# Padding the rows of weight, input and squared-activation buffers of a two-layer encoder kernel

## The chip, the cores and the metric

The kernel runs on one core of one Trainium2 chip. The metric is the device time of one execution in microseconds (us), as a median of repeated runs. Beside it stands one profiled execution, from which every duration of a single instruction is read.

Engine names as in the profile: PE is TensorE doing matrix products, PEld is TensorE loading the stationary operand of a product, DVE is VectorE, ACT is ScalarE, POOL is GpSimd, SP is SyncE, which issues most DMA transfers. A name such as L125 is a line of the kernel file.

## What is computed

The reference is a small sequence model in float32: 512 tokens, width 1024, two layers, each a token mixer and an MLP, both with a norm ahead and a residual behind.

```python
for i in range(DEPTH):                       # DEPTH = 2
    h = _rmsnorm(x, norm_mix[i])
    if i % 2 == 0:                           # differential attention and pooling
        ...
        x = x + jnp.concatenate([a_out, b_out], axis=-1) @ ab_w_out[e]
    else:                                    # gated linear attention
        x = x + _gla_mixer(h, gla_w_in[o], ..., gla_w_out[o])
    h = _rmsnorm(x, norm_ffn[i])
    x = x + jnp.square(jax.nn.relu(h @ ffn_w1[i])) @ ffn_w2[i]   # 1024 -> 4096 -> 1024
return _rmsnorm(x, norm_final)
```

Nearly all arithmetic lies in products with weights. The two MLPs alone hold 2 x 2 x 1024 x 4096 weights.

## The kernel before

**Products in three passes.** A weight product is made from float32r operands. Each operand is split in a high part and a low part: `wh` and `wl` for weights, `ah` and `al` for inputs. Each product is then the sum of three matrix products, `wh*ah + wh*al + wl*ah`. They are the lines L125, L126 and L127 of the helper `mm3`. The stationary operand is a block of 128x128 of `wh` or `wl`; it is loaded by an LDWEIGHTS ahead of its own product, while the product before it still runs. The moving operand is a whole tile `ah` or `al` with 512 columns, one for each token.

**One output tile.** `proj_T` makes 128 output features for all tokens: it goes over eight blocks `kb` of 128 input features, three products each, so 24 products go to one PSUM bank. `proj_tok` (L150 to L152) makes the opposite layout for the attention values, with `ah` or `al` stationary and `wh` or `wl` moving.

**Weights.** `Stream.next` hands out halves of a unit of 1 MB. The unit is loaded by a DMA from SP into one of two `wraw` buffers. `split_w` makes `wh` on ACT (L103) and `wl` on DVE (L104). There are four `wh` and four `wl` buffers of 1024 numbers each, so several halves are ready ahead.

**The MLP** (`ffn`). In four chunks, eight output tiles of the first weight are made from the 8 pairs `ah`, `al`. Each result is put through relu and squared and split in two tiles of the row `r16` (L425 to L428), so a chunk fills 16 tiles of `r16`. Then eight output tiles of the second weight are made with these `r16` tiles as moving operands. In the very last chunk (`last_chunk`) this second half is done in two halves of 256 tokens. So the program has long stretches in which PE reads `ah` and `al`, and stretches of 192 products in which it reads `r16`. Trace names cut off buffer numbers, so `r16` and `r8` both appear as `r`.

**Layer mixers.** Attention and pooling in layer 0, gated linear attention in layer 1, are made of weight products with other, smaller products put between them (for instance sums over partitions, L182 and L183, which multiply a temporary tile with the ones matrix `onesr`). The low-rank gate of layer 1 (L522) is a run of 16 products whose stationary operand is an `r8` tile and whose moving operands are `ah` and `al`.

**Order and places.** A tile scheduler orders each engine's instructions; `soon` raises the priority of what PE waits for. Buffers of one tag form a row in SBUF, a fixed stretch of bytes in each partition; the rows stand one behind the other, and a tag's buffers have equal distances. The allocation helper is

```python
def T(shape, tag, bufs, dt=F32):
    cnt[0] += 1
    return sb.tile(shape, dt, tag=tag, bufs=bufs, name=f"{tag}_{cnt[0]}")
```

`w_tiles` asks it for `wh` and `wl` (4 buffers of 4096 bytes each per partition), `act_tiles` for `ah` and `al` (12 of 2048 bytes each), `row16` for `r16` (16 of 2048 bytes). All these sizes are multiples of 512 bytes, so all buffers of a row begin at the same remainder modulo 512. In the built program the remainders are 128 for every buffer of `wh`, `wl`, `ah` and `al`, also for `tmp` and `onesr`, and 256 for every buffer of `r8` and `r16`. A 128x128 block within `wh` or `wl` begins a multiple of 512 bytes behind its buffer's start.

Of the kernel before, what the change touches and what calls it, by code (L numbers as in the profile page):

```python
# [17 lines left out]
S = 512  # L18
# [9 lines left out]

# columns of the packed parameter array
C_MIX0, C_FFN0, C_MIX1, C_FFN1, C_FIN = 0, 8, 16, 24, 32  # L30
# [5 lines left out]
def trunk(ctx: ExitStack, tc: tile.TileContext, xT, par, lvl, lam4, wqk0, wu0, wv0, poolw, wo0,  # L36
          wgk, wup, wqk1, wv1, wg1, wo1, w1a, w2a, w1b, w2b, outT):
    nc = tc.nc
# [3 lines left out]
    cnt = [0]  # L42

    def T(shape, tag, bufs, dt=F32):
        cnt[0] += 1
        return sb.tile(shape, dt, tag=tag, bufs=bufs, name=f"{tag}_{cnt[0]}")

    # buffers by how long they are held: a row of 8 and a row of 16
    def row8(n=S, dt=F32):
# [17 lines left out]

    # what the tensor engine waits for goes ahead of the rest
    def soon(n=300):
        return tc.high_priority(n)  # L70

    # ---- parameters, inputs and the first unit of weights
    prm = T([P, N_PAR], "par", 1)
# [16 lines left out]

    # ---- weight streaming: raw float32 units, split into two parts of 12 bits
    def load(src):
# [14 lines left out]
    class Stream:  # L107
        """Halves of the units of one weight array, in order."""

# [19 lines left out]
    def proj_T(w, act, ts=slice(0, S)):  # L129
        """[128 features, tokens] from a half unit [128, 8, 128] and split inputs."""  # L130
        hi, lo = w
        ps = PS("mm", (P, ts.stop - ts.start))
        for kb in range(KB):
            c = slice(kb * P, (kb + 1) * P)
            ah, al = act[kb]
            mm3(ps, (hi[:, c], lo[:, c]), (ah[:, ts], al[:, ts]), kb == 0, kb == KB - 1)
        return ps

    def proj_tok(stream, act):
        """Four [128 tokens, 512 features] results from half units [128, 2, 512]."""  # L140
        pss = [PS("mm") for _ in range(NT)]
        for pair in range(KB // 2):
            wh, wl = stream.next()
            for t in range(NT):
                ts = slice(t * P, (t + 1) * P)
                for j in range(2):
                    kb = 2 * pair + j
                    c = slice(j * S, (j + 1) * S)
                    ah, al = act[kb]
                    PE.matmul(pss[t], ah[:, ts], wh[:, c], start=kb == 0, stop=False)  # L150
                    PE.matmul(pss[t], al[:, ts], wh[:, c], start=False, stop=False)  # L151
                    PE.matmul(pss[t], ah[:, ts], wl[:, c], start=False, stop=kb == KB - 1)  # L152
        return pss

    def split_scaled(src, col):
        """Parts of src * (a value per partition)."""
        ah, al = act_tiles()
        A.activation(ah, src, AF.Copy, scale=col)
        V.scalar_tensor_tensor(out=al, in0=src, scalar=col, in1=ah.bitcast(F32), op0=ALU.mult, op1=ALU.subtract)
        return ah, al  # L160
# [7 lines left out]
    def spread(r):  # L168
        """Values per token [128, n] along the free axis of every partition, in PSUM."""
        n = r.shape[-1]  # L170
        ps = PS("ax", (P, n * P))
        for t in range(n):
            PE.matmul(ps[:, t * P:(t + 1) * P], r[:, t:t + 1].to_broadcast([P, P]), ident, start=True, stop=True)
        return ps

    def col_sums(sq, c):
        """Sums over all partitions, on every partition, of a tile to which c is added."""
        n = sq.shape[-1]
        ps, hi, lo = PS("ax", (P, n)), tmp(n, F32R), tmp(n, F32R)
        A.activation(hi, sq, AF.Copy)  # L180
        V.scalar_tensor_tensor(out=lo, in0=sq, scalar=c, in1=hi.bitcast(F32), op0=ALU.add, op1=ALU.subtract)
        PE.matmul(ps, ones_r, hi, start=True, stop=False)  # L182
        PE.matmul(ps, ones_r, lo, start=False, stop=True)  # L183
        return ps
# [7 lines left out]
    def rsqrt(r, v, inv):  # L192
        """(v * inv) ** -0.5: a first value by logarithm, then one Newton step."""
        A.activation(r, v, AF.Ln, scale=inv)
        A.activation(r, r, AF.Exp, scale=-0.5)
        return newton(r, v, inv, tmp(r.shape[-1]))

    def neg_recip(r, v, inv):
        """-1 / (v * inv), in the same way."""
        t = tmp(r.shape[-1])  # L200
        A.activation(r, v, AF.Ln, scale=inv)
        A.activation(r, r, AF.Exp, scale=-1.0)
        V.scalar_tensor_tensor(out=t, in0=v, scalar=inv, in1=r, op0=ALU.mult, op1=ALU.mult)
        V.scalar_tensor_tensor(out=r, in0=t, scalar=-2.0, in1=r, op0=ALU.add, op1=ALU.mult)
        return r

    class Norm:
        """Sums of squares over the features of x, tile by tile."""

# [24 lines left out]
    def per_token(rb):  # L234
        """One row of rb as [128 tokens, 4]."""
        ps = PS("ax", (P, NT))
        for t in range(NT):
            PE.transpose(ps[:, t:t + 1], rb[0:1, t * P:(t + 1) * P], ident[0:1, 0:1])
        r = T([P, NT], "rtok", 1)
        V.tensor_copy(r, ps)  # L240
        return r

    # ================= layer 0: attention and pooling =================
    act = []
# [16 lines left out]
    rb = nrm.rb()  # L261

    # lambda on every partition
    l4 = tmp(256)
# [25 lines left out]
    def scores(h, qts):  # L290
        """Score blocks of 128 queries each, masked, in two banks; minus their scaled maxima."""
        banks = [PS("ax"), PS("ax")]
# [18 lines left out]
    def softmax(h, qt, views, neg):  # L311
        """p1 - lambda * p2, transposed, into the head's tiles."""
        n = (qt + 1) * P
# [29 lines left out]
    def attend(h):  # L343
        """The products with the values, normalised."""
        po = PS("ax")
# [26 lines left out]

    # pooling branch
    pw = tmp2().rearrange("p (g c) -> p g c", g=4)
# [24 lines left out]
    def add_out(arr, src, col):  # L399
        """x += (split inputs) @ weights; the next block's inputs and norm."""  # L400
        st = Stream(arr)
# [50 lines left out]
    def last_chunk(s2, a, rb2):  # L452
        """The end of the last block by halves of the tokens, each with its final norm."""
        for half in range(2):
# [34 lines left out]

    # constants of layer 1  # L490
    lv = T([P, NLEV + 1, P], "lvl", 1, U8)
# [10 lines left out]

    # ================= layer 1: gated linear attention =================
    with soon(800):
        smask = row8()
        G.memset(smask, 1.0)
        G.memset(smask.rearrange("p (c t) -> p c t", t=P)[:, :, 0:1], 0.0)
        # gate weights: both parts of the 16 columns side by side, so two passes make all the products;
        # four copies of them, for the stacked product of the up-projection
        gk2 = [row8(dt=F32R).rearrange("p (k a b) -> p k a b", k=4, a=4) for _ in range(2)]  # L510
        for i in range(2):
            src = gkr[:, 4 * i:4 * i + 4, :, :]
            A.activation(gk2[i][:, :, :, 0:16], src, AF.Copy)
            V.tensor_tensor(gk2[i][:, :, :, 16:32], src, gk2[i][:, :, :, 0:16].bitcast(F32), ALU.subtract)
        # rows 0-63: the weights' high part, rows 64-95: the low part
        wu = row8(dt=F32R)
# [7 lines left out]
    rb = nrm.rb()  # L524
    # rows 0-31 and 64-95: the high part of the gate's input, rows 32-63: the low part
    gkf = tmp2()
# [37 lines left out]
    def weights(h):  # L564
        """Products within chunks, and the factors across them, of one head."""
        ps = proj_T(st.next(), act)
# [8 lines left out]
        b3 = b.rearrange("p (c t) -> p c t", t=P)  # L575
        # across chunks
        e = row16()
# [16 lines left out]
        kdt.append(kd)  # L594
        # within chunks: the diagonal, then pairs (second half, first half) of ever smaller blocks
        at = row16()
# [6 lines left out]
        for l in range(NLEV - 1):  # L603
# [12 lines left out]
            if s >= 16:  # L616
                # whole blocks, which start at partitions that a product can be put at
                for p0 in range(0, P, 2 * s):
# [7 lines left out]
            for c in range(NT):  # L626
# [3 lines left out]
                              psl.rearrange("p (c t) -> p c t", t=P))  # L630
        # neighbours, as the diagonal: the products' sums over the features
        d = tmp(S // 2)
# [23 lines left out]
    def outputs(h):  # L656
        """Transposed outputs of one head, normalised: two tiles [128 features, tokens]."""
        half, hh = divmod(h, 2)
# [34 lines left out]

    # the parts of the heads, in the order that keeps every engine supplied
    for h in range(3):
# [28 lines left out]

# ---- layout on the host
def _blocks_T(w):
    """Rows in blocks of 1024, columns in units of 256: [units, 128, 2, 8 * 128]."""
    k, n = w.shape
# [4 lines left out]
def _blocks_tok(w):  # L733
    """Columns in blocks of 512, rows in units of 512: [units, 128, 2, 2 * 512]."""
    n = w.shape[1]
# [64 lines left out]
```

## Time and profile before

| | us |
|---|---|
| median of 3 runs | 1136.92 |
| lowest and highest run | 1136.45, 1137.26 |
| span of the profiled execution, first to last instruction | 1135.0 |
| PE busy | 1118.5 |
| PEld busy | 904.5 |
| DVE busy | 641.5 |
| ACT busy | 468.2 |
| POOL busy | 7.2 |

The profiled execution is one run; its time is its span and the little that lies ahead of and behind the instructions. Its span is 1.9 us under the median of the runs. Busy time of PE counts the stretch in which any product is under way. One product is recorded with about 0.39 us, but products overlap in the pipeline: the next one begins 0.23 us later. What counts for the time is therefore the distance from one product's start to the next one's start; it is called the **pitch** below, and is read from the timeline, which prints starts to 0.01 us.

### The profile page before, as it was taken

What the parts mean: (1) busy time and instruction counts of PE and PEld (TensorE: products, weight loads), DVE (VectorE), ACT (ScalarE), POOL (GpSimd) and SP (SyncE); (2) the same over time, 40 slices, a digit from 0 to 9 for tenths busy, and PEclk for the clock granted to TensorE, in tenths of its full rate; (3) what the DMA queues carried; (4) which work ended last, traced back from release to release, by engine and by line L of the source; (5) the groups of instructions that cost most, each with busy time, mean ns of one, the idle gap of its engine ahead of it and who ended that gap; (6) DMA issues with size and microseconds to landing.
All of it is one profiled execution on the core that took longest, in us unless ns stands there. A gap on an engine that the chain in (4) does not pass through costs nothing.

```text
span 1135.0 us, 13269 instructions
## 1 busy us (share of the span) xinstructions
PE 1118.5 (99%) x5312; PEld 904.5 (80%) x5312; DVE 641.5 (57%) x1024; ACT 468.2 (41%) x748; POOL 7.2 (1%) x26
## 2 busy tenths in 40 slices
PE   8999999999999999999999999999999999999996
PEld 6676778888888888888777788888888888888896
DVE  7757866423433455456898867555323434455485
ACT  7445544323322422334645466434323313312463
POOL 0000000000000000000000000000000000000001
PEclk9999999999999999999999999999999999999998
DMA  7221233232222323222121312232232323223252
GB/s 247 80 90 38 84 109 111 74 111 79 107 103 84 111 74 111 81 106 92 58 75 38 113 38 74 74 112 88 98 109 77 111 74 112 91 96 107 79 187 75
DMA packets 19229, 107.21 MB, mean 94 GB/s; under 512 B 2048, under 2 KB 5120, under 8 KB 7008
## 3 DMA queue, kind: packets, MB, share of 16 engines
q1 hardware_dynamic: 19024, 106.34, 26.9%
q8 instruction: 42, 0.69, 0.2%
q14 instruction: 19, 0.16, 0.0%
q10 hardware_dynamic: 144, 0.03, 0.0%
HBM read 104.26 MB, written 2.10 MB: 94 GB/s over the span
## 4 chain that ended last, share of the span: by engine, by line
PE 92%; DVE 2%; issue 2%; ACT 2%; DMA 1%; SPq 0%; POOL 0%; POOLq 0%; DVEq 0%; ACTq 0%
PE psmm L127 26%; PE psmm L126 26%; PE psmm L125 26%; PE psmm L150 2%; PE psmm L152 2%; PE psmm L151 2%; PE psax L301 1%; PE psax L628 1%; PE psax L621 1%; PE psax L347 1%; DMA wraw<-in_wqk 1%; PE psax L182 1%; PE psax L678 0%; PE psax L663 0%; PE psax L329 0%
## 5 line engine op out<-in xcount | busy, mean ns | idle before, releaser
L103 ACT ACTIVATE wh<-wraw 128x1024 fp32r<-128x1024 f32 x190 | 200.9, 1059 | 517.6 <-PE psmm L126 480.1
L104 DVE TENSOR_TENSOR wl<-wraw,wh 128x1024 fp32r<-128x1024 f32 x190 | 232.2, 1223 | 264.3 <-ACT wh L103 263.6
L125 PE MATMUL psmm<-ah,wh 128*128 128x512 f32 x864 | 339.6, 393 | 4.9 <-ACT wh L250 4.9
L126 PE MATMUL psmm<-al,wh 128*128 128x512 f32 x864 | 339.4, 393 | 0.0
L127 PE MATMUL psmm<-ah,wl 128*128 128x512 f32 x864 | 338.9, 392 | 0.0
L126 PE MATMUL psmm<-r,wh 128*128 128x512 f32 (+1 forms) x576 | 213.0, 370 | 0.1
L125 PE MATMUL psmm<-r,wh 128*128 128x512 f32 (+1 forms) x576 | 213.1, 370 | 0.0
L127 PE MATMUL psmm<-r,wl 128*128 128x512 f32 (+1 forms) x576 | 213.0, 370 | 0.0
L125 PEld LDWEIGHTS psmm<-ah,wh 128*128 128x128 f32 x864 | 162.7, 188 | 41.1 <-ACT wh L250 5.6
L126 PEld LDWEIGHTS psmm<-al,wh 128*128 128x128 f32 x864 | 162.7, 188 | 36.5 <-issue 2.1
L127 PEld LDWEIGHTS psmm<-ah,wl 128*128 128x128 f32 x864 | 162.8, 188 | 35.7 <-issue 1.6
L126 PEld LDWEIGHTS psmm<-r,wh 128*128 128x128 f32 x576 | 108.2, 188 | 20.7 <-DVE r L428 0.3
L127 PEld LDWEIGHTS psmm<-r,wl 128*128 128x128 f32 x576 | 108.2, 188 | 20.4
L125 PEld LDWEIGHTS psmm<-r,wh 128*128 128x128 f32 x576 | 108.1, 188 | 20.4
L439 DVE TENSOR_TENSOR r<-r,psmm 128x512 f32<-128x512 f32 x32 | 22.0, 687 | 88.7 <-PE psmm L127 88.7
L428 DVE TENSOR_TENSOR r<-tmp,r 128x512 fp32r<-128x512 f32 x64 | 44.3, 692 | 6.5
L427 DVE TENSOR_TENSOR tmp<-tmp 128x512 f32<-128x512 f32 x64 | 43.8, 684 | 0.0
L426 ACT ACTIVATE r<-tmp 128x512 fp32r<-128x512 f32 x64 | 40.5, 634 | 2.0
L150 PE MATMUL psmm<-wh,ah 128*128 128x512 f32 x96 | 39.1, 407 | 0.0
L151 PE MATMUL psmm<-wh,al 128*128 128x512 f32 x96 | 38.5, 401 | 0.0
L152 PE MATMUL psmm<-wl,ah 128*128 128x512 f32 x96 | 38.2, 398 | 0.0
L425 ACT ACTIVATE tmp<-psmm 128x512 f32<-128x512 f32 x64 | 36.9, 577 | 0.0
(183 smaller groups left out, 813.0 us busy)
## 6 DMA issues: line engine op xcount, KB each, us to landing
wraw<-in_w2b SPq DMA_DIRECT2D x20, 1024.0 KB, 4.8
wraw<-in_w1a SPq DMA_DIRECT2D x16, 1024.0 KB, 4.8
wraw<-in_w2a SPq DMA_DIRECT2D x16, 1024.0 KB, 4.8
wraw<-in_w1b SPq DMA_DIRECT2D x16, 1024.0 KB, 4.8
wraw<-in_wo SPq DMA_DIRECT2D x8, 1024.0 KB, 4.7
wraw<-in_wqk SPq DMA_DIRECT2D x7, 1024.0 KB, 4.9
wraw<-in_wv SPq DMA_DIRECT2D x6, 1024.0 KB, 4.7
wraw<-in_wg SPq DMA_DIRECT2D x4, 1024.0 KB, 4.9
```

Of the source, the lines that this page charges most:

```text
L103: A.activation(hi, src, AF.Copy)
L104: V.tensor_tensor(lo, src, hi.bitcast(F32), ALU.subtract)
L125: PE.matmul(ps, wh, ah, start=first, stop=False)
L126: PE.matmul(ps, wh, al, start=False, stop=False)
L127: PE.matmul(ps, wl, ah, start=False, stop=last)
L150: PE.matmul(pss[t], ah[:, ts], wh[:, c], start=kb == 0, stop=False)
L151: PE.matmul(pss[t], al[:, ts], wh[:, c], start=False, stop=False)
L152: PE.matmul(pss[t], ah[:, ts], wl[:, c], start=False, stop=kb == KB - 1)
L425: A.activation(r, ps, AF.Relu)
L426: A.activation(hi, r, AF.Square)
L427: V.tensor_tensor(q, r, r, ALU.mult)
L428: V.tensor_tensor(lo, q, hi.bitcast(F32), ALU.subtract)
```

## The change

The helper `T` takes a table of paddings, in numbers of 4 bytes. A buffer of `wh` and `wl` gets 16 numbers (64 bytes) more than its 1024, a buffer of `ah`, `al` and `r16` 24 numbers (96 bytes) more than its 512. The tile handed out is a slice without the padding. To make room, the area in SBUF that is kept for descriptors of DMAs issued by GpSimd shrinks from 16384 to 2048 bytes per partition. This kernel issues its DMAs from SP and ACT.

```diff
+    PAD = {"wh": 16, "wl": 16, "ah": 24, "al": 24, "r16": 24}
+
     def T(shape, tag, bufs, dt=F32):
         cnt[0] += 1
-        return sb.tile(shape, dt, tag=tag, bufs=bufs, name=f"{tag}_{cnt[0]}")
+        pad = PAD.get(tag)
+        if pad is None:
+            return sb.tile(shape, dt, tag=tag, bufs=bufs, name=f"{tag}_{cnt[0]}")
+        p, n = shape
+        full = {"wh": 1024, "wl": 1024}.get(tag, S) + pad
+        return sb.tile([p, full], dt, tag=tag, bufs=bufs, name=f"{tag}_{cnt[0]}")[:, 0:n]
...
-    nc = bacc.Bacc("TRN2", target_bir_lowering=False, num_devices=1)
+    nc = bacc.Bacc("TRN2", target_bir_lowering=False, num_devices=1, dynamic_dma_scratch_size=2048)
```

The rest of the diff takes out comments and docstrings. Lines of the helpers move down by 8: `mm3` is L133 to L135 afterwards, `split_w` L111 and L112.

In the built programs every engine has the same instructions in the same order with the same waits, before and after. What differs are start addresses in SBUF:

| row | start modulo 512 before | start modulo 512 after |
|---|---|---|
| `wh` (4) | 128 | 128, 192, 256, 320 |
| `wl` (4) | 128 | 384, 448, 0, 64 |
| `ah` (12) | 128 | 128, 224, 320, 416, 0, 96, 192, 288, 384, 480, 64, 160 |
| `al` (12) | 128 | 256, 352, 448, 32, 128, 224, 320, 416, 0, 96, 192, 288 |
| `r16` (16) | 256 | 0, 96, 192, 288, 384, 480, 64, 160, 256, 352, 448, 32, 128, 224, 320, 416 |
| `r8` (8) | 256 | 0 |
| `tmp`, `onesr`, `wraw`, `x` | 128 | 384, 128, 128, 128 |

A number that is used below is the **distance**: the start of the moving operand of a product minus the start of the stationary operand that is loaded while this product runs (that of the next product), modulo 512 bytes. Counted over the built programs:

```
products of float32r                     distance before           distance after
moving operand 512 columns, not r16      0: 2848 of 2865           all 16 multiples of 32, each 133 to 255 of 2865
moving operand r16, 512 columns          128: 1343 of 1344         all 16 multiples of 32, each 73 to 96 of 1344
moving operand r16, 256 columns          128: 380 of 380           15 of the 16 multiples of 32, each 11 to 48 of 380
```

Of the 17 others of the first row, 16 have distance 384: they stand around the gate's run L522, whose moving operands lie at 128 and whose stationary ones lie at 256.

## The prediction

> **What bounds the kernel now.** I read the page first: span, busy times, clock, and the chain of work that ended last.
>
> ```profile
> span 1135.0 us, 13269 instructions
> PE 1118.5 (99%) x5312; PEld 904.5 (80%) x5312; DVE 641.5 (57%) x1024; ACT 468.2 (41%) x748; POOL 7.2 (1%) x26
> PEclk9999999999999999999999999999999999999998
> PE 92%; DVE 2%; issue 2%; ACT 2%; DMA 1%; SPq 0%; POOL 0%; POOLq 0%; DVEq 0%; ACTq 0%
> ```
>
> PE is busy 99% of the span and is 92% of the chain, at full granted clock but for the last slice. So time is won or lost only where the pitch of the products changes, that is the distance from one start to the next. The groups of instructions (count, busy time and mean of one, then the idle time before them and its releaser) say which products these are, and whether the splitting of the weights is in their way.
>
> ```profile
> L103 ACT ACTIVATE wh<-wraw 128x1024 fp32r<-128x1024 f32 x190 | 200.9, 1059 | 517.6 <-PE psmm L126 480.1
> L104 DVE TENSOR_TENSOR wl<-wraw,wh 128x1024 fp32r<-128x1024 f32 x190 | 232.2, 1223 | 264.3 <-ACT wh L103 263.6
> L125 PE MATMUL psmm<-ah,wh 128*128 128x512 f32 x864 | 339.6, 393 | 4.9 <-ACT wh L250 4.9
> L125 PE MATMUL psmm<-r,wh 128*128 128x512 f32 x448 | 176.9, 395 | 0.0
> L125 PE MATMUL psmm<-r,wh 128*128 128x256 f32 x128 | 36.1, 283 | 0.0
> ```
>
> L126 and L127 have as many as L125: 3 x 864 = 2592 products with `ah` or `al` moving, 3 x 448 = 1344 with `r16`, 3 x 128 = 384 of half length. L125 never waits but for 4.9 us at the start, whereas L103 waits 517.6 us, 480.1 of them for PE to give a buffer back. The splits run ahead of PE.
>
> The third view is the timeline of PE alone, at the place where the first MLP goes over from `ah` and `al` to `r16` (start, duration, instruction):
>
> ```profile
> 223.51 0.39 PE L126 MATMUL psmm<-al,wh 128*128 128x512 f32 x1
> 223.74 0.39 PE L127 MATMUL psmm<-ah,wl 128*128 128x512 f32 x1
> 223.97 0.40 PE L125 MATMUL psmm<-r,wh 128*128 128x512 f32 x1
> 224.20 0.39 PE L126 MATMUL psmm<-r,wh 128*128 128x512 f32 x1
> 224.42 0.40 PE L127 MATMUL psmm<-r,wl 128*128 128x512 f32 x1
> 224.66 0.39 PE L125 MATMUL psmm<-r,wh 128*128 128x512 f32 x1
> 224.89 0.40 PE L126 MATMUL psmm<-r,wh 128*128 128x512 f32 x1
> 225.13 0.39 PE L127 MATMUL psmm<-r,wl 128*128 128x512 f32 x1
> 225.36 0.40 PE L125 MATMUL psmm<-r,wh 128*128 128x512 f32 x1
> ```
>
> Ahead of 223.97 the steps are 0.23; behind it 0.23, 0.22, 0.24, 0.23, 0.24, 0.23: another rhythm, that swings between two values. Over whole stretches (start and end, their length, then busy time and count on PE, PEld, DVE, ACT and POOL, clock, DMA share and GB/s) this gives exact pitches:
>
> ```profile
> 269.45:312.29 42.84, 42.84 (x190) 35.47 (x189) 18.86 (x22) 16.09 (x24) 0.00 (x0) 1.00 0.29 98
> sum 459.00, PE 459.00 PEld 380.07 DVE 232.93 ACT 187.61 POOL 0.00; mean PE 57.38 PEld 47.51 DVE 29.12 ACT 23.45 POOL 0.00
> 223.97:268.76 44.79, 44.79 (x194) 36.05 (x192) 11.10 (x10) 13.00 (x18) 0.00 (x0) 1.00 0.27 94
> sum 313.53, PE 313.53 PEld 252.29 DVE 132.59 ACT 84.14 POOL 0.63; mean PE 44.79 PEld 36.04 DVE 18.94 ACT 12.02 POOL 0.09
> ```
>
> The first row is eight output tiles of a first MLP weight, without their first three products: 8 x 24 - 3 = 189 products in 42.84 us, a pitch of **226.7 ns** (the 190th counted began before the stretch). The first sum is over eight such stretches, all with nothing but this even rhythm: 459.0 us, so 459.0 / 0.2267 = 2025 products. The third row is eight output tiles of a second weight: 192 products in 44.79 us, **233.3 ns**. The last row adds up all seven such stretches, 1344 products.
>
> One engine, one clock, instructions of one shape, no wait, and yet two pitches. What differs is the place of the operands: by the table of the change the distance is 0 in the one kind and 128 in the other. The gate's run has it the other way round, stationary at 256 and moving at 128:
>
> ```profile
> 533.97 0.39 PE L522 MATMUL psmm<-al,r 128*128 128x512 f32 x1
> 534.20 0.40 PE L522 MATMUL psmm<-ah,r 128*128 128x512 f32 x1
> 534.44 0.39 PE L522 MATMUL psmm<-al,r 128*128 128x512 f32 x1
> 534.67 0.40 PE L522 MATMUL psmm<-ah,r 128*128 128x512 f32 x1
> ```
>
> Steps of 0.23, 0.24, 0.23: the swinging rhythm, with `ah` and `al` moving. So it is not a matter of `r16`, but of the two places taken together. I read this as the loading of the next stationary operand getting in the way of the stream of the moving one, by an amount that hangs on the distance.
>
> At distance 0 the even rhythm has to be found first. Behind an interruption it looks like this:
>
> ```profile
> 564.91 0.40 PE L127 MATMUL psmm<-ah,wl 128*128 128x512 f32 x1
> 565.14 0.40 PE L125 MATMUL psmm<-ah,wh 128*128 128x512 f32 x1
> 565.38 0.39 PE L126 MATMUL psmm<-al,wh 128*128 128x512 f32 x1
> 565.60 0.39 PE L127 MATMUL psmm<-ah,wl 128*128 128x512 f32 x1
> ...
> 567.23 0.39 PE L127 MATMUL psmm<-ah,wl 128*128 128x512 f32 x1
> ```
>
> There are ten steps from 564.91 to 567.23 (the rows between begin at 565.83, 566.07, 566.29, 566.53, 566.76 and 566.99), so the mean is **232 ns**, with single steps from 0.22 to 0.24. All ten have distance 0. Only then come the steps of 226.7. So 226.7 is no property of one product: it is a state that a row of products of one and the same distance falls into, and stays in.
>
> **The change part by part.** No instruction, order or wait changes. The work is priced by the pitch alone.
>
> *Products with `ah` or `al` moving.* After the change their distance takes all 16 multiples of 32 evenly and is another one at nearly every product, so a state that needs one lasting distance is not reached. Only distances 0, 128 and 384 are in this trace; for the 13 others there is no row. Bounds from the nearest rows, where the trace holds starts to 1 ns: 224 ns (the least step, from 224.20 to 224.42, shown as 0.22) and 238 ns (the greatest, from 224.42 to 224.66, shown as 0.24). I take 232, the unsettled run above, since the products there have the same form and stream the same tiles, and only the settling is missing. Cost: 2025 x (232 - 226.7) = **+10.7 us**. At the bounds: 2025 x (224 - 226.7) = -5.5 and 2025 x (238 - 226.7) = +22.9. The remaining products of this kind stand between other work, much of it unsettled already; I leave them as they are.
>
> *Products with `r16` moving.* They are spread over the distances as well, and I take the same 232: 1344 x (232 - 233.3) = **-1.7 us**. At the bounds: -12.5 and +6.3.
>
> *Half-length products at the end.* Their pitch is read from a stretch of the last half chunk:
>
> ```profile
> 1080.64 0.28 PE L127 MATMUL psmm<-r,wl 128*128 128x256 f32 x1
> ...
> 1081.95 0.28 PE L126 MATMUL psmm<-r,wh 128*128 128x256 f32 x1
> ```
>
> Eleven steps in 1.31 us are 119 ns. They swing already, so I take no change; 384 x 2 ns = 0.8 us either way.
>
> *Splits and the other users of the padded tiles.* L103 takes 1059 ns and L104 1223 ns; whether ACT and DVE mind the new places no row shows. With 5% more or less on both, (200.9 + 232.2) x 0.05 = 22 us of work would shift, all beside PE: L103 has 517.6 us of waiting ahead of it. I take 0. If that cover were gone, 22 us would be the price.
>
> *The smaller area for DMA descriptors.* The list of DMA issues names only the queues of SP and ACT, none of POOL. I take 0 on both sides.
>
> Sum: 10.7 - 1.7 = +9.0 us on the span of 1135.0, so 1144.0; with the 1.9 us by which the median of the runs is longer, **1146 us**, 0.8% slower.
>
> **A rule against it.** The Trainium skill, page "SBUF — State Buffer", section "Who interferes with whom", gives TensorE two independent read ports, one for the moving operand and one for the load, and says that it never waits on anyone. By that rule the places of the operands are no matter and the sum is 0 us, where it is +9.0 by the rows. The trace disagrees with it in so far as 226.7 and 233.3 ns stand side by side for products of one form without a wait.
>
> **The rivals.**
>
> *Faster: the distances not yet seen are cheaper.* The trace's evidence is for distance 0 and for 128 on either side; if the two streams mostly collide when they are close or a multiple of 128 apart, 13 of 16 distances may be free of it, and spreading dilutes the two bad ones. Its place is the same 2025 + 1344 products. The mean pitch of these is (459.0 + 313.5) / 3369 = 229.3 ns, so it decides the sign from there: below 229.3 the change gains. At 224 for all it gives -5.5 - 12.5 = -18 us, 1119. Lower is hard to see: a full product costs 226.7 and a half one 119, so the second 256 columns cost 108 and the first 256, during which the load runs, 11 more (the two pitches are of distance 0 and 128, so this is an estimate). If those 11 vanished, the pitch would be 216, the sum 3369 x (216 - 229.3) = -45 us, and the time 1092. Against it: steps of 216 occur nowhere in these rows, and the two distances 128 and 384, far from 0, are both dearer than the settled 0, not cheaper.
>
> *Nothing.* The two pitches come from something else, for instance from the row that an operand belongs to and not from where it begins; then places are no matter, the change does not do what it says, and the time stays 1137. The rule of the page "SBUF — State Buffer" above would have this result, in the Trainium skill's words because the two ports are independent. Against it stands the gate's run, where `ah` and `al` swing too.
>
> *Dearer throughout.* Each change of distance from product to product throws the rhythm off anew, and the greatest step becomes the usual one: 238 for all, +22.9 + 6.3 = +29 us, 1166. For it: in the unsettled run the step from 565.14 to 565.38 is such a one. Against it: the next step is a short one of 0.22, to 565.60.
>
> **How the numbers follow.** Forecast 0.53 (1139 to 1156, as the pitch comes out between 230 and 235), dearer throughout 0.07, faster 0.28, nothing 0.12. This measurement can tell about 0.2% from no change, 2.3 us. Forecast and dearer make slower 0.60, the third faster 0.28, the fourth same 0.12. The likeliest is 1146. The range reaches down to 1119, where every pitch is the least step seen, and up to 1160, a pitch of 236 throughout; what lies beyond on either side I give 0.08 to 0.10.
>
> **What would show it.** In the profile of the changed kernel the first-weight stretch, 42.84 us now, should take 189 x 232 = 43.8 us and the second-weight stretch, 44.79 now, 192 x 232 = 44.5: the two kinds become alike. The steps in the timeline should no longer be even anywhere, and repeat, if at all, with the tile's 24 products. L103 should still wait hundreds of us for PE, and L125 still begin without waiting. The prediction is wrong if the even rhythm survives, if steps well under 224 ns are common, or if PE gains idle time ahead of L125, which would mean that the splits became the bound.

## The result and the profile after

| | before | after |
|---|---|---|
| median (us) | 1136.95 (1136.45 to 1137.26, 4 runs) | 1145.24 (1144.70 to 1145.43, 4 runs) |
| ratio to before, 95% interval | | 1.0072 (1.0058 to 1.0086) |
| span of the profiled execution (us) | 1135.0 | 1143.3 |

The change makes the kernel 0.7% slower. The page after, in the lines that answer to those shown of before (`mm3` is now L133 to L135, `split_w` L111 and L112):

```profile
span 1143.3 us, 13269 instructions
PE 1126.9 (99%) x5312; PEld 904.1 (79%) x5312; DVE 642.2 (56%) x1024; ACT 468.6 (41%) x748; POOL 7.3 (1%) x26
L111 ACT ACTIVATE wh<-wraw 128x1024 fp32r<-128x1024 f32 x190 | 201.0, 1060 | 525.6 <-PE psmm L134 487.5
L112 DVE TENSOR_TENSOR wl<-wraw,wh 128x1024 fp32r<-128x1024 f32 x190 | 232.3, 1224 | 270.7 <-ACT wh L111 270.0
L133 PE MATMUL psmm<-ah,wh 128*128 128x512 f32 x864 | 343.0, 397 | 5.2 <-ACT wh L258 5.2
```

The count of instructions is the same, the splits take 1060 and 1224 ns (1059 and 1223 before), and they wait longer for PE, not PE for them. PE's busy time has grown by 8.4 us and the span by 8.3. Nearly all of it is pitch. The following rows are the same stretches as before, found by their products: the first row is the first-weight stretch of 189 products, the second row the second-weight stretch of 192, then the sum over the eight stretches of the first kind (2025 products) and over the seven of the second (1344):

```profile
271.91:315.64 43.73, 43.73 (x190) 35.47 (x189) 18.87 (x22) 16.11 (x24) 0.00 (x0) 1.00 0.27 96
226.64:271.22 44.58, 44.58 (x193) 36.06 (x192) 11.10 (x10) 13.01 (x18) 0.00 (x0) 1.00 0.27 95
sum 468.69, PE 468.69 PEld 380.11 DVE 232.90 ACT 187.68 POOL 0.00; mean PE 58.59 PEld 47.51 DVE 29.11 ACT 23.46 POOL 0.00
sum 311.53, PE 311.53 PEld 252.40 DVE 132.65 ACT 84.17 POOL 0.63; mean PE 44.50 PEld 36.06 DVE 18.95 ACT 12.02 POOL 0.09
```

The first kind went from 459.0 to 468.7 us, +9.7, a mean pitch of 231.5 ns. The second went from 313.5 to 311.5, -2.0, a mean of 231.8. Together that is +7.7 of the 8.3 us. The even rhythm is gone; this is PE's timeline within a first-weight stretch, where before every step was 0.22 or 0.23:

```profile
290.65 0.39 PE L133 MATMUL psmm<-ah,wh 128*128 128x512 f32 x1
290.88 0.39 PE L134 MATMUL psmm<-al,wh 128*128 128x512 f32 x1
291.11 0.40 PE L135 MATMUL psmm<-ah,wl 128*128 128x512 f32 x1
291.35 0.39 PE L133 MATMUL psmm<-ah,wh 128*128 128x512 f32 x1
291.57 0.40 PE L134 MATMUL psmm<-al,wh 128*128 128x512 f32 x1
291.81 0.39 PE L135 MATMUL psmm<-ah,wl 128*128 128x512 f32 x1
292.04 0.40 PE L133 MATMUL psmm<-ah,wh 128*128 128x512 f32 x1
```

The steps are 0.23, 0.23, 0.24, 0.22, 0.24, 0.23.

### The profile page after: what moved, and what is told of

Same layout as the page of the kernel before. It is cut to its first block, busy times and chain, and to the rows that moved or that the text cites. A ratio compares the mean times of both kernels' runs of the same rounds, so it can differ in the third digit from the quotient of the medians.

```text
span 1143.3 us, 13269 instructions
## 1 busy us (share of the span) xinstructions
PE 1126.9 (99%) x5312; PEld 904.1 (79%) x5312; DVE 642.2 (56%) x1024; ACT 468.6 (41%) x748; POOL 7.3 (1%) x26
## 2 busy tenths in 40 slices
DMA packets 19229, 107.21 MB, mean 94 GB/s; under 512 B 2048, under 2 KB 5120, under 8 KB 7008
## 4 chain that ended last, share of the span: by engine, by line
PE 93%; issue 2%; DVE 2%; ACT 1%; DMA 1%; POOL 0%; SPq 0%; POOLq 0%; DVEq 0%
PE psmm L135 26%; PE psmm L134 26%; PE psmm L133 26%; PE psmm L158 2%; PE psmm L159 2%; PE psmm L160 2%; PE psax L309 1%; PE psax L636 1%; PE psax L629 1%; PE psax L355 1%; PE psax L686 1%; DMA wraw<-in_wqk 1%; PE psax L190 1%; PE psax L688 0%; PE psax L337 0%
## 5 line engine op out<-in xcount | busy, mean ns | idle before, releaser
L111 ACT ACTIVATE wh<-wraw 128x1024 fp32r<-128x1024 f32 x190 | 201.0, 1060 | 525.6 <-PE psmm L134 487.5
L112 DVE TENSOR_TENSOR wl<-wraw,wh 128x1024 fp32r<-128x1024 f32 x190 | 232.3, 1224 | 270.7 <-ACT wh L111 270.0
L133 PE MATMUL psmm<-ah,wh 128*128 128x512 f32 x864 | 343.0, 397 | 5.2 <-ACT wh L258 5.2
L135 PE MATMUL psmm<-ah,wl 128*128 128x512 f32 x864 | 342.4, 397 | 0.0
L135 PE MATMUL psmm<-r,wl 128*128 128x512 f32 (+1 forms) x576 | 212.5, 369 | 0.0
L133 PE MATMUL psmm<-r,wh 128*128 128x512 f32 (+1 forms) x576 | 212.3, 369 | 0.0
L133 PEld LDWEIGHTS psmm<-ah,wh 128*128 128x128 f32 x864 | 162.8, 188 | 44.9 <-ACT wh L258 6.2
L135 PEld LDWEIGHTS psmm<-ah,wl 128*128 128x128 f32 x864 | 162.6, 188 | 39.3 <-issue 1.6
L135 PEld LDWEIGHTS psmm<-r,wl 128*128 128x128 f32 x576 | 108.2, 188 | 19.7
L133 PEld LDWEIGHTS psmm<-r,wh 128*128 128x128 f32 x576 | 108.2, 188 | 19.7
L435 DVE TENSOR_TENSOR tmp<-tmp 128x512 f32<-128x512 f32 x64 | 43.8, 684 | 0.0
```

The lines of the kernel that those rows point to most:

```text
L111: A.activation(hi, src, AF.Copy)
L112: V.tensor_tensor(lo, src, hi.bitcast(F32), ALU.subtract)
L133: PE.matmul(ps, wh, ah, start=first, stop=False)
L135: PE.matmul(ps, wl, ah, start=False, stop=last)
L435: V.tensor_tensor(q, r, r, ALU.mult)
```

## Experiments

All kernels start from the kernel before. A gap is a small tile that is never used; it moves the rows behind it. "First stretch" and "second stretch" are the two stretches of 189 and 192 products shown above, found again in each run. The rows of the view by stretches are quoted for each kernel, first stretch first.

### Every distance at 0

```diff
+    T([P, 96], "gap2", 1)
     st = Stream(wqk0, 2)
```

The gap of 96 numbers (384 bytes) stands ahead of `r8` and `r16`.

> The kernel before, with nothing but a gap of 384 bytes ahead of the rows r8 and r16, so that they begin at 128 modulo 512 too and every distance is 0. Theory (settling: products at one lasting distance fall into a rhythm that belongs to that distance): the second-weight stretches, 44.79 us before, fall into the 226.7 ns rhythm and take 43.5 us; 1344 x 6.6 ns = 8.9 us less than before, 1128 us, ratio 0.992. Rival (the two pitches belong to the rows, not to where they begin): stretch 44.79 us and 1137 us unchanged.

```profile
268.34:311.18 42.84, 42.84 (x190) 35.47 (x189) 18.86 (x22) 16.11 (x24) 0.00 (x0) 1.00 0.28 98
224.14:267.66 43.52, 43.52 (x193) 36.04 (x192) 11.10 (x10) 12.99 (x18) 0.00 (x0) 1.00 0.27 97
```

Time 1128.16 us, ratio 0.9921 (0.9906 to 0.9936), faster than both kernels. The second stretch fell from 44.79 to 43.52 us, 226.7 ns for each product, as forecast. No instruction is other than before; `r8`, `r16` and the small rows behind them begin 384 bytes further on. So the two pitches do not belong to the rows, and the rival falls. The Trainium skill (page "SBUF — State Buffer", section "Who interferes with whom") says that TensorE never waits on anyone. The 8.6 us that a gap alone gains here are against that, as far as it is read as "the places of the operands are no matter".

### The parts of the change, one at a time

Each of the three kernels has one of these lines, the part of the padding table that is named, and the smaller descriptor area:

```diff
+        pad = {'r16': 24}.get(tag, 0)
...
+        pad = {'ah': 24, 'al': 24}.get(tag, 0)
...
+        pad = {'wh': 16, 'wl': 16}.get(tag, 0)
```

The squared activations alone:

> The part of the change on r16 alone (24 numbers of padding) and the smaller descriptor area; weights and inputs as before. Theory: first-weight stretch stays 42.84 us, second-weight stretch falls from 44.79 to 44.5 us (192 x 231.8 ns, as in the changed kernel), 2 us less, 1135 us. Rival (the descriptor area or something else than distances makes the changed kernel slower): the first-weight stretch gets longer here too, and the time is over 1137.

```profile
269.52:312.38 42.86, 42.86 (x190) 35.47 (x189) 18.86 (x22) 16.09 (x24) 0.00 (x0) 1.00 0.28 98
224.24:268.82 44.58, 44.58 (x193) 36.05 (x192) 11.11 (x10) 13.00 (x18) 0.00 (x0) 1.00 0.28 95
```

1134.82 us, ratio 0.9981 (0.9972 to 0.9990). The first stretch is where it was, so the descriptor area costs nothing; the second fell a little. This part of the change is a small gain.

The inputs alone:

> The part of the change on ah and al alone (24 numbers of padding) and the smaller descriptor area; weights as before, r16 unpadded, which puts it at distance 384. Theory: the whole loss lies here: first-weight stretch 43.8 us (189 x 231.6 ns), second-weight stretch stays at 44.8 us since 384 swung like 128 in the gate's run; some 10 to 11 us more, 1147 to 1148 us, slower than the changed kernel. Rival (padding of the weights is what costs): first-weight stretch 42.84 us, 1137 us.

```profile
272.13:315.87 43.74, 43.74 (x191) 35.48 (x190) 18.86 (x22) 16.11 (x24) 0.00 (x0) 1.00 0.27 96
226.65:271.44 44.79, 44.79 (x193) 36.05 (x192) 11.09 (x10) 12.99 (x18) 0.00 (x0) 1.00 0.28 94
```

1147.52 us, ratio 1.0092 (1.0077 to 1.0107). The loss of the change is here, and with the gain of the part before, 1.0092 x 0.9981 = 1.0073, as good as the result of the change, 1.0072. In this kernel `r16` lies at the lasting distance 384, and the second stretch takes 44.79 us, 233.3 ns for each product, as at 128.

The weights alone:

> The part of the change on wh and wl alone (16 numbers of padding) and the smaller descriptor area; ah, al and r16 as before. Within an output tile the distance now changes only between wh and wl (by 256), in a pattern that repeats every three products; it shifts by 64 from tile to tile. Theory: such a short repeat can settle again, to a pitch of its own for each buffer; first-weight stretch between 42.8 and 44.2 us, with long runs of a repeating rhythm inside a tile. Rival (every single distance has its price, whatever stands around it): the mean of the changed kernel by distance, 230 to 234 ns at once and without a settled run, first-weight stretch 43.7 us, 1145 us.

```profile
271.30:314.89 43.59, 43.59 (x191) 35.54 (x189) 18.87 (x22) 16.11 (x24) 0.00 (x0) 1.00 0.28 97
226.32:270.62 44.30, 44.30 (x194) 36.09 (x193) 11.10 (x10) 12.99 (x18) 0.00 (x0) 1.00 0.28 95
```

1141.93 us, ratio 1.0042 (1.0025 to 1.0059). The padding of the weights is enough to lose by; on top of that of the inputs it adds nothing, as far as the ratios tell. Within an output tile a rhythm settles here after some products, and each `wh` and `wl` buffer has its own. At 1 ns, the steps of three tiles that follow one another from 153.8 us on, by the remainder at which their `wh` buffer begins:

```
192: 233 234 233 233 234 233 233 234 233 233 234 233 233 234 233 233 234 233 233 234 233 233 234 233
128: 236 224 231 236 228 233 230 227 227 226 227 227 226 227 227 226 227 227 226 227 227 226 227 226
320: 229 232 226 229 231 226 229 232 226 229 232 226 229 231 226 229 232 226 229 232 226 229 231 233
```

In the second tile the distances are 0 and 256, and the even 226.7 comes back after seven steps. That speaks for settling, and against one price for each distance. In all three tiles the moving operands begin at 128, and yet the pitch goes with the weight buffer. So it is not the place of the moving operand alone, but its place relative to the stationary ones.

### Other lasting distances

Gaps ahead of `ah` and ahead of `r8` (here for 32 and 64), so that each kind of product has one distance from end to end:

```diff
+    T([P, 8], "gap1", 1)
     for f in range(KB):
...
+    T([P, 104], "gap2", 1)
     st = Stream(wqk0, 2)
...
-    nc = bacc.Bacc("TRN2", target_bir_lowering=False, num_devices=1)
+    nc = bacc.Bacc("TRN2", target_bir_lowering=False, num_devices=1, dynamic_dma_scratch_size=2048)
```

> The kernel before with gaps between rows and the smaller descriptor area, so that ah and al lie at one lasting distance of 32, r16 at 64. Theory (settling): in both kinds of stretches a short rhythm repeats without end, each with a pitch of its own between 224 and 238 ns: first-weight stretch 42.3 to 45.0 us, second-weight stretch 43.0 to 45.7. Rival (only distance 0 is cheap, all others cost the 232 ns that the changed kernel shows): 43.8 and 44.5 us, without a repeating rhythm.

```profile
271.90:316.00 44.10, 44.10 (x190) 35.43 (x189) 18.86 (x22) 16.10 (x24) 0.00 (x0) 1.00 0.28 96
227.26:271.21 43.95, 43.95 (x194) 36.06 (x193) 11.10 (x10) 13.02 (x18) 0.00 (x0) 1.00 0.28 96
```

> The same with lasting distances 96 for ah and al, 160 for r16. Theory: repeating rhythms; 96 has the dearest mean but one in the changed kernel (233.2 ns), so first-weight stretch at or over 44.0 us; second-weight stretch between 43.0 and 45.7. Rival: 43.8 and 44.5 us, no repeating rhythm.

```profile
273.51:317.62 44.11, 44.11 (x190) 35.49 (x189) 18.85 (x22) 16.08 (x24) 0.00 (x0) 1.00 0.28 96
227.82:272.80 44.98, 44.98 (x193) 36.19 (x192) 11.10 (x10) 12.98 (x18) 0.00 (x0) 1.00 0.28 94
```

> The same with lasting distances 256 for ah and al, 192 for r16. Theory: repeating rhythms; 256 has the cheapest mean in the run with only the weights padded (227.7 ns), so first-weight stretch near 42.9 us; second-weight stretch near 44.8 (192 had 233.4 ns there). Rival: 43.8 and 44.5 us, no repeating rhythm.

```profile
269.71:312.56 42.85, 42.85 (x191) 35.49 (x189) 18.86 (x22) 16.08 (x24) 0.00 (x0) 1.00 0.28 98
224.22:269.02 44.80, 44.80 (x194) 35.95 (x192) 11.09 (x10) 13.00 (x18) 0.00 (x0) 1.00 0.28 94
```

> The same with lasting distances 480 for ah and al, 320 for r16. Theory: repeating rhythms; 320 had 228.1 ns with only the weights padded, so second-weight stretch near 43.8 us; first-weight stretch between 42.3 and 45.0. Rival: 43.8 and 44.5 us, no repeating rhythm.

```profile
273.34:317.44 44.10, 44.10 (x191) 35.52 (x189) 18.87 (x22) 16.08 (x24) 0.00 (x0) 1.00 0.28 96
227.84:272.64 44.80, 44.80 (x194) 36.34 (x192) 11.10 (x10) 12.98 (x18) 0.00 (x0) 1.00 0.27 94
317.44:361.38 43.94, 43.94 (x193) 36.08 (x192) 15.92 (x17) 9.60 (x11) 0.00 (x0) 1.00 0.28 97
406.19:450.14 43.95, 43.95 (x194) 36.08 (x192) 25.87 (x34) 11.04 (x13) 0.63 (x2) 1.00 0.28 96
```

The times, of one execution each, are 1144.88, 1154.33, 1135.85 and 1147.72 us in this order, beside 1137.44 of the kernel before. The forecasts for 96, 256 and 192 hold. That for 320 does not, in the first second-weight stretch: 44.80 us instead of 43.8. But the last two rows, the next second-weight stretches of the same run, have 43.94 and 43.95. At one and the same distance, stretches of equal work on PE fell into two rhythms, 233.3 and 228.9 ns, and each kept its own for 192 products. The addresses do not decide between the two: in the built program the stretch from 406.19 us on has the same operand addresses in the same order as that from 227.84 us on. So the pitch hangs on the distance and on something else, perhaps the state that a stretch began with. What sets it is not shown. It is the first second-weight stretch that is slow, in layer 1 as in layer 0, and there ACT takes the results out of PSUM, where DVE does it in the others.

The rival's numbers, 43.8 and 44.5 us, came nowhere. But it holds a part of the truth: of eight new distances only 256 is as cheap as 0, and five cost as much as 128 or more from end to end. The following pitches in ns are set side by side; the middle column pairs the trace's products of the changed kernel with those of its built program, where the distance of each is known. Ten of the 16 distances are listed.

```
distance   in the changed kernel, ah and al   lasting
   0             230.4 (178 products)          226.7
  32             231.4 (150)                   233.3
  64             231.8 (200)                   228.9
  96             233.2 (187)                   233.4
 128             231.1 (157)                   233.3
 160             231.9 (163)                   234.3
 192             231.7 (169)                   233.3
 256             230.3 (195)                   226.7
 320             230.9 (128)                   233.3 or 228.9
 480             230.3 (250)                   233.3
```

A product at distance 0 costs 226.7 ns among its like and 230.4 when its neighbours have other distances. With the neighbours mixed, the pitch hangs less on the distance: the middle column lies between 230.3 and 233.2 ns, the right one between 226.7 and 234.3. The dearest of the six that are not listed is 352, with 234.1 ns in the changed kernel.

One thing these runs do not separate. Wherever one distance lasts, a product's own stationary operand begins at the same remainder modulo 256 as the next one's. So they do not tell which of the two the moving operand's place must agree with.

### Padding by 256 bytes

All five rows padded as in the change, but by 64 numbers, with the smaller descriptor area and a gap of 128 bytes ahead of `r8`; nearly every distance is then 0 or 256, in changing order.

```diff
+        pad = {'wh': 64, 'wl': 64, 'ah': 64, 'al': 64, 'r16': 64}.get(tag, 0)
...
+    T([P, 32], "gap2", 1)
```

> All five rows padded as in the change, but by 256 bytes (64 numbers) each, with a gap ahead of r8 and r16 that puts every distance at 0 or 256, about half and half, in changing order. Theory (the two streams meet in a pattern that repeats every 256 bytes, and a lasting remainder modulo 256 is enough to settle): first-weight stretch 42.84 us and second-weight stretch 43.5 us, 1128 us, as with all distances at 0; then it is the 64 and 96 bytes that harm and not the padding as such. Rival (any change of distance from product to product unsettles the rhythm): 43.8 and 44.5 us, near 1146 us.

```profile
267.97:310.81 42.84, 42.84 (x190) 35.47 (x189) 18.85 (x22) 16.12 (x24) 0.00 (x0) 1.00 0.29 98
223.77:267.29 43.52, 43.52 (x193) 36.04 (x192) 11.10 (x10) 12.99 (x18) 0.00 (x0) 1.00 0.28 97
```

1128.38 us, ratio 0.9928 (0.9911 to 0.9945). That is the time of the kernel with the gap of 384 bytes alone, 1128.16 us. So the gain comes from the gap, which brings `r16` to the cheap distances, and padding by 256 bytes costs nothing beside it. Neighbouring buffers lie at other multiples of 256 bytes here, and the even rhythm takes no notice. It is not spreading as such that harms, but leaving the remainder modulo 256 that the moving and the stationary operand had in common.

### Half the load

From the kernel with all distances at 0. The products for half of the output features are left out in six of the eight blocks:

```diff
+            m = P if kb in (0, KB - 1) else 64
-            c = slice(kb * P, (kb + 1) * P)
+            c = slice(kb * P, kb * P + m)
             ah, al = act[kb]
-            mm3(ps, (hi[:, c], lo[:, c]), ...)
+            mm3(ps[0:m], (hi[:, c], lo[:, c]), ...)
```

> The kernel with all distances at 0, but in six of the eight blocks of each output tile the stationary operand has only its first 64 columns; the products for the other 64 output features are left out there. The moving operand still has 512 columns. Theory (a product loses time because the load of the next stationary operand reads beside its stream): with loads of half the length the loss above 213.3 ns (half of the 426.7 ns that the first, slow products take) falls from 13.3 ns towards half, mean pitch near 220 ns in a stretch, first-weight stretch between 41.3 and 42.2 us. Rival (the loss belongs to the product itself, to its start or its end, whatever is loaded beside it): pitch 226.7 ns and stretches of 42.84 and 43.5 us as with full loads.

```profile
269.64:312.96 43.32, 43.32 (x190) 27.87 (x189) 18.85 (x22) 16.11 (x24) 0.00 (x0) 1.00 0.29 97
224.97:268.96 43.99, 43.99 (x193) 28.39 (x192) 11.10 (x10) 12.98 (x18) 0.00 (x0) 1.00 0.28 96
```

The time was 1134.52 us in one execution, beside 1136.73 of the kernel before and 1128.16 with full loads at distance 0. PEld's busy time (the second in the row) fell from 35.47 to 27.87 us, so the loads are shorter; but the stretch got longer, 43.32 us, a pitch of 229.2 ns. Both forecasts miss. The timeline among the short loads:

```profile
275.61 0.39 PE L127 MATMUL psmm<-ah,wl 128*64 128x512 f32 x1
275.83 0.39 PE L125 MATMUL psmm<-ah,wh 128*64 128x512 f32 x1
276.06 0.40 PE L126 MATMUL psmm<-al,wh 128*64 128x512 f32 x1
276.29 0.39 PE L127 MATMUL psmm<-ah,wl 128*64 128x512 f32 x1
276.52 0.40 PE L125 MATMUL psmm<-ah,wh 128*64 128x512 f32 x1
276.76 0.39 PE L126 MATMUL psmm<-al,wh 128*64 128x512 f32 x1
276.99 0.39 PE L127 MATMUL psmm<-ah,wl 128*64 128x512 f32 x1
277.21 0.39 PE L125 MATMUL psmm<-ah,wh 128*64 128x512 f32 x1
```

Seven steps in 1.60 us are 229 ns, uneven though the distance is 0. So the loss does not shrink with the number of columns loaded. Among the six products with full loads that stand ahead of these, from 273.78 to 275.14 us, the steps are still 227 ns. The edit changes two things at once: a product with half the stationary columns also makes half the output. So this run does not tell whether the shorter load or the product itself upset the rhythm. What exactly the stream of the moving operand meets stays open.

## Why the prediction was right

**The bound.** PE's pitch is nearly all that moved: +9.7 - 2.0 us of 8.3 in the two kinds of long stretches. There is no new wait; the one at the start grew from 4.9 to 5.2 us. The little that is left lies outside these stretches, among products that the prediction left as they were. The splits' time is unchanged to 1 ns, so the cover of 517.6 us was not needed.

**Products with `ah` or `al`.** The term was 2025 x (232 - 226.7) = +10.7 us; it measured +9.7, at 231.5 ns. That products of these changing distances miss the even rhythm was foreseen rightly. That the size came out so well was partly luck: the 232 ns were ten steps behind an interruption, all at distance 0 and one of them a sum over partitions (L183), and no row showed that a mixture of distances would have the same pitch. The padding of the inputs alone brings this loss, that of the weights alone most of it (43.74 and 43.59 us in the first stretch).

**Products with `r16`.** The term was -1.7 us; it measured -2.0 with 231.8 ns. Alone it makes the kernel faster, 0.9981.

**Half-length products, descriptor area.** Both were taken as 0, and nothing speaks against it. From the start of the first half-length product to that of the last it is 47.3 us before and 47.1 after. With `r16` alone padded and the area shrunk, the first stretch stays at 42.86 us.

**Where the reasoning was too simple.** Two points of the way there did not hold in full. First, I read 226.7 ns as what any lasting distance might settle to, with 128 as an exception. The runs show the reverse: most lasting distances settle at 233 to 234 ns, dearer than the mixture, and 0 and 256, with 64 and 320 in between, are the exceptions. Nor does the even rhythm need one lasting distance: with 0 and 256 in changing order it holds (42.84 us). The change loses because it leaves the cheap distance 0, and not because a mixture is the worst case. That also answers the rival "faster": distances not seen before were not free, they were mostly as dear as 128. Second, I put the loss down to the loading of the next operand beside the stream. The run with half the load does not bear this out, and it cannot rule it out either, since it changed the product too; the partner in the collision was not found.

**The rivals.** "Nothing" falls with the gap that turned 233.3 into 226.7 ns. "Dearer throughout" at 238 came nowhere; the dearest lasting pitch is 234.3.

## What to carry to other kernels

Where PE is busy nearly all the time, measure the distance from one product's start to the next and compare it between stages: two values for one shape, without a wait, can come from where the buffers begin. Here 384 bytes of gap, so that the moving and the stationary operand begin at the same remainder modulo 256, were worth 0.8%. This holds for products of 512 columns in this kernel; those of 256 columns go by other distances (next section). Padding against conflicts is no safe habit: by 64 and 96 bytes it cost 0.7% here, by 256 bytes nothing, and an experiment with a gap is cheap.

## What the runs showed of the hardware that was not expected

A row of products at one distance can settle in more than one rhythm and keep it: at distance 320, 233.3 ns in one stretch and 228.9 in the next. Half-length products show two rhythms as well. In the kernel with lasting distance 64 a run in the first half of the last chunk has

```profile
1104.27 0.28 PE L125 MATMUL psmm<-r,wh 128*128 128x256 f32 x1
...
1106.20 0.28 PE L127 MATMUL psmm<-r,wl 128*128 128x256 f32 x1
```

These are 17 steps in 1.93 us, 113.5 ns for 256 columns; before, it was 119. In the second half, at the same distance, it is

```profile
1110.80 0.28 PE L127 MATMUL psmm<-r,wl 128*128 128x256 f32 x1
...
1111.86 0.28 PE L127 MATMUL psmm<-r,wl 128*128 128x256 f32 x1
```

with nine steps in 1.06 us, 118 ns. And 0 is not the cheap distance at this length. In the kernel with every distance at 0 the last chunk has

```profile
1080.22 0.28 PE L125 MATMUL psmm<-r,wh 128*128 128x256 f32 x1
...
1082.14 0.28 PE L126 MATMUL psmm<-r,wh 128*128 128x256 f32 x1
```

with 16 steps in 1.92 us, 120 ns, a little more than the 119 of before at 128. At full length no lasting pitch under 226.7 ns was found in any run, although 216 was the estimate without any loss.
